# Two heads of the neighbourhood attention on the two column halves of the array, q and k stored as parts, and four smaller moves

## The chip, the cores and the metric

The kernel runs on one core of a Trainium2 chip. The metric is the device time of one execution in microseconds (us). The engines are PE (TensorE; PEld is its weight load), DVE (VectorE), ACT (ScalarE), POOL (GpSimd) and SP, whose queue issues the DMAs.

## The reference, cut to what matters

Two layers over 1024 latent and 256 context tokens of width 1024. Layer 0 mixes with attention: four differential heads over all 1280 keys, and eight neighbourhood heads (width 64) whose queries see an 8 x 16 window of a grid 64 wide plus the 256 context keys:

```python
s = concat([q·k_window * scale + bias, q·k_ctx * scale])   # one softmax over both
p = softmax(s)
out = p[:n_loc] @ v_window + p[n_loc:] @ v_ctx
```

Layer 1 mixes with a recurrent block: a projection, a width-4 convolution, two sigmoid gates for each of two directions, a scan each way, and the product with a GELU lane. Each mixer and each convolutional FFN is modulated by vectors made from `c` by a 1024 x 6144 matrix per layer (`ada_w`), and wrapped in a residual LayerNorm. All is float32.

## The kernel before

Products that need float32 accuracy are made from parts: x = h + l, with h rounded to the array's fast type (`fp32r`) on ACT and l = x - h on DVE or POOL (`split`, L101). A projection then takes three matmuls (`mm3`, L121). The score matmuls of the attention take two, with q's high part in the first 64 rows and its low part in the last 64 (`heads`, L479; `scores`, L531).

Stages in order of time: modulation rows and the v projection; the q/k projection (`qkv`, from L436); the differential units; the neighbourhood units; the output projection (`proj_ln`); the FFN of layer 0; the recurrent block (`rnn`); its output projection; the FFN of layer 1.

*The q/k projection* has 16 blocks of 128 output channels (L446). A block splits its weight (L447: ACT, then POOL), runs 8 x 3 matmuls for each of three column chunks into PSUM banks taken in turn, evicts on ACT into the one tile `q` (L463), rotates the first eight blocks on DVE and POOL (L468 to L471), and stores `q` to DRAM (L472). Three steps of `ada` are laid between: each loads a 512 KB row of `ada_w` through the same ring of three tiles as the weights, and DVE multiplies and sums it twice (L205).

*Heads* are loaded from DRAM ahead of their use, by `ahead`: each of q and k twice, into both halves of the partitions, then cast on DVE (L500, L503) and subtracted on POOL (L501, L505).

*A neighbourhood unit* is one head m of a pair, for 128 queries (j), and is a generator of six steps: scores and the maximum (DVE L1449, L1450); exp on ACT with the sum, and the division of p by it on DVE (L1469); six or seven transposes of p on PE; their eviction; the product with v; its eviction into 64 rows of `o` (L1507). v's 64 columns are the stationary operand, so the product uses 64 columns of the array: columns 0 to 63 for m = 0, the others for m = 1. In each turn of the loop from L587 PE gets the scores of unit i+2, the transposes of i-1 and the product of i-2.

*The recurrent block* makes, for each n of 8, four gate lanes by sigmoid (L1147) from one PSUM region of three banks, then two scans; lanes 2 and 3 have one buffer each (L1122), which n+1 takes after the last reader of n (L1178 on POOL, L1179 on DVE).

Each engine runs its queue in order. The order is chosen by a planner that models times, except where `in_turn` (L90) fixes it: in attention all of PE's, ACT's, DVE's and POOL's instructions are in turn, each on its engine, but not the first weights of the output projection (`w_ao`), which the planner put between the q/k projection and the first differential units. The loads and stores share SP's queue.

Of the kernel before, what the change touches and what calls it, by code (L numbers as in the profile page):

```python
# [26 lines left out]
P = 128  # L27
# [30 lines left out]
class Kernel:  # L58
    def __init__(self, nc, tc, es, a):
        self.nc, self.tc, self.a, self.es = nc, tc, a, es  # L60
        self.turns = {}
        self.pe_key = self.ld_key = None
        self.rooms = 0
        self.cast = None
        self.const = self.pool(es, "const", 1)
# [3 lines left out]
        self.qk_s = [d.tile([P, T], F32, name=f"qk_s{i}", tag=f"qk_s{i}") for i in range(16)]  # L69
# [283 lines left out]
    def qkv(self, esa):  # L353
        nc, a = self.nc, self.a
        with ExitStack() as es:
# [80 lines left out]
            with ExitStack() as es1:  # L436
                qp = self.pool(es1, "qkproj", 1)
                more = self.ada(qp, [(0, p) for p in (2, 3, 4, 5)] + [(1, 0), (1, 1)], 0)
                cos = qp.tile([P, TL], F32, name="cos")
                sin = qp.tile([P, TL], F32, name="sin")  # L440
                cyc = itertools.cycle((4, 6, 7))
                self.spare((5,))
                self.ld(cos, a["cos"])
                self.ld(sin, a["sin"])
                shuf = [(i + 16) % 32 for i in range(32)]
                for n, i in enumerate((0, 4, 1, 5, 2, 6, 3, 7, 8, 12, 9, 13, 10, 14, 11, 15)):  # L446
                    w = self.weight(a["w_qk"][i])  # L447
                    if n == 3:
                        self.pool_p = self.pool(esa, "weights", 1, side="right")
                        self.diff = DiffAttention(self)  # L450
                    if n == 15:

                        cyc = itertools.cycle((6, 7))
                        self.pe_key = "att_pe"
                        self.first = self.diff.unit(0, 0)
                        for _ in range(4):
                            next(self.first)
                    q = qp.tile([P, T], F32, name="q", tag="q")
                    scale = 0.125 if i // 4 in (0, 2) else 1.0
                    for c0, cn in CHUNKS:  # L460
                        ps = self.banks(next(cyc))
                        self.block(ps[:, :cn], w, c0, cn)
                        nc.scalar.mul(q[:, c0:c0 + cn], ps[:, :cn], scale)  # L463
                        if n:
                            next(more, None)
                    if i < 8:
                        rot = qp.tile([P, TL], F32, name="rot", tag="rot")
                        nc.vector.stream_shuffle(rot, q[:, :TL], shuf)  # L468
                        nc.vector.tensor_mul(rot, rot, sin)
                        nc.gpsimd.tensor_mul(q[:, :TL], q[:, :TL], cos)  # L470
                        nc.vector.tensor_add(q[:, :TL], q[:, :TL], rot)  # L471
                    self.st(self.qk_s[i], q)  # L472
                self.pe_key = None
                for _ in more:
                    pass
            self.fold(0, 0, 0, 0, 3, 4)


    def heads(self, n, out, sub=None):  # L479

        nc = self.nc
        pool = self.sets[n % 2]
        iq, ik = (n, 4 + n) if n < 4 else (4 + n, 8 + n)
        parts = []
        v = pool.tile([P, NT, P], F32, name="v", tag="v")
        out.append((parts, v))
        for m in range(2):

            rows = slice(m * 64, m * 64 + 64)
            qr = pool.tile([P, T], F32, name="qr", tag="qr")  # L490
            kr = pool.tile([P, T], F32, name="kr", tag="kr")
            for t_, i in ((qr, iq), (kr, ik)):
                self.ld(t_[0:64], self.qk_s[i][rows])
                self.ld(t_[64:128], self.qk_s[i][rows])
# [4 lines left out]
            yield  # L499
            self.dve(nc.vector.tensor_copy(qs, qr))  # L500
            self.pl(nc.gpsimd.tensor_sub(qs[64:128], qr[64:128], qs[64:128].bitcast(F32)))  # L501
            yield
            self.dve(nc.vector.tensor_copy(kh, kr))  # L503
            if sub is None:
                self.pl(nc.gpsimd.tensor_sub(kl, kr, kh.bitcast(F32)))  # L505
            else:
                sub.tensor_sub(kl, kr, kh.bitcast(F32))
        self.ld(v, self.v_s[:, :, n * P:(n + 1) * P].rearrange("t p e -> p t e"))

    def dve(self, ins):  # L510
# [26 lines left out]
    def attention(self):  # L537
# [3 lines left out]
        with ExitStack() as es:  # L541
# [45 lines left out]
            for i in range(nd, len(units) + 2):  # L587
                s(i + 2)
                if i == nd:
                    s(i - 1)  # L590
                s(i + 1)
                t = i - 1
                if t >= nd:
                    s(t, 2)
                    f(i, 2)
                if i < len(units):
                    n.ahead(*units[i][1:])
                if i == nd:
                    s(nd - 1, 2)
                    done(nd - 1)  # L600
                elif t > nd:
                    s(t - 1, 2)

    def turn_out(self, o, blk, scale, bank):

# [74 lines left out]
    def proj_ln(self, src, w, nk, l, which, nt, x_in, x_out, nx, fold, sizes, more=(), held={},  # L680
# [8 lines left out]
        with ExitStack() as es:  # L689
# [14 lines left out]
            for size in sizes:  # L704
# [11 lines left out]
                for k in range(nk):  # L716
# [3 lines left out]
                    if gt is None and k == (nk - 1 if tail else 0):  # L720
# [6 lines left out]
                    wh, wl = self.weight(w[k], (P, D), nc.vector)  # L727

                    first = early and t0 == 0
                    if tail and t0 == 0:  # L730
# [358 lines left out]
    def rnn(self, left):  # L1089
# [32 lines left out]
        def lane(i, n):  # L1122

            j = {0: 0, 1: 1, 4: 2}.get(i)
            if j is not None and n % 2:
                return self.aring.tile([P, T], F32, name="lane", tag=f"a{j}")
            return self.ln.tile([P, T], F32, name="lane", tag=f"y{i}")

# [8 lines left out]
        def gates(n, g, xs, x, yg):  # L1137
# [157 lines left out]
class DiffAttention:  # L1295
    def __init__(self, kn):
        self.kn = kn
        self.heads, self.outs = [], {}
        for _ in kn.heads(0, self.heads, kn.nc.vector):
            pass  # L1300
        self.next = iter(())

# [9 lines left out]
    def unit(self, h, b):  # L1312
# [35 lines left out]
        wT = pool.tile([P, T], F32, name="wT", tag="wT", bufs=2)  # L1348

        def turn(g):  # L1350
            pt = kn.banks((6, 7, 6)[g])
# [36 lines left out]
class NatAttention:  # L1388
# [42 lines left out]
    def unit(self, pr, j, m):  # L1431
# [35 lines left out]
        for u in range(nu):  # L1467
            sl = slice(u * n // nu, (u + 1) * n // nu)
            kn.dve(nc.vector.tensor_scalar_mul(p[:, sl], p[:, sl], rr[:, u:u + 1]))  # L1469
        yield  # L1470
        pT = pool.tile([P, T], F32, name="wT", tag="wT", bufs=2)
        self.pair = 10 - self.pair
        ba, bb = kn.banks(self.pair), kn.banks(self.pair + 1)
        work = ((ba, 0, 4, 0), (bb, 4, 4 if j == NTL else 2, 4 * P if j == NTL else nr * GW))
# [12 lines left out]
            self.outs[pr] = pool.tile([P, T], F32, name="o", tag="o", bufs=2)  # L1487
        o = self.outs[pr]
        if j == NTL:
            for u in range(4):  # L1490
                hs, qs = slice(u % 2 * 64, u % 2 * 64 + 64), slice(u // 2 * P, u // 2 * P + P)
                for k in range(2):
                    kn.mm(ba[hs, qs], v[:, NTL + k, hs], pT[:, (2 * u + k) * P:(2 * u + k + 1) * P],
                          start=k == 0, stop=k == 1)
            yield
            kn.act(o[:, TL:], ba[:, :TC], AF.Copy)
# [5 lines left out]
        hs = slice(m * 64, m * 64 + 64)  # L1502
# [102 lines left out]
```

## Time and profile before

| | us |
|---|---|
| median of 3 runs | 3009.2 (3004.59 to 3010.11) |
| the profiled execution, its own time | 3005.08 |
| its span | 3003.3 |
| PE busy in the span | 2859.1 (95%) |
| DVE, ACT, POOL busy | 2061.9, 1475.3, 931.3 |

Busy time of PE includes matmuls that run at the lower of its two clocks. The stages need different engines, so each is read by itself, by windows of the trace.

### The profile page before, as it was taken

What the parts mean: (1) busy time and instruction counts of PE and PEld (TensorE: products, weight loads), DVE (VectorE), ACT (ScalarE), POOL (GpSimd) and SP (SyncE); (2) the same over time, 40 slices, a digit from 0 to 9 for tenths busy, and PEclk for the clock granted to TensorE, in tenths of its full rate; (3) what the DMA queues carried; (4) which work ended last, traced back from release to release, by engine and by line L of the source; (5) the groups of instructions that cost most, each with busy time, mean ns of one, the idle gap of its engine ahead of it and who ended that gap; (6) DMA issues with size and microseconds to landing.
All of it is one profiled execution on the core that took longest, in us unless ns stands there. A gap on an engine that the chain in (4) does not pass through costs nothing. (4 is left out here: it accounts for less than half of the span.)

```text
span 3003.3 us, 38303 instructions
## 1 busy us (share of the span) xinstructions
PE 2859.1 (95%) x14430; PEld 2367.8 (79%) x14430; DVE 2061.9 (69%) x2743; ACT 1475.3 (49%) x2358; POOL 931.3 (31%) x636
## 2 busy tenths in 40 slices
PE   8987988889999999999999999999989999999998
PEld 5876777778887888778888888777767888888876
DVE  6079759988866787875556645566688977777364
ACT  4211136666666664344444434466767554454232
POOL 4134204543300015354430000244311366761001
PEclk9998999999999999999999999999989999999999
DMA  6365542223208413632126646311146122225452
GB/s 227 128 183 194 198 158 71 71 62 87 61 29 279 175 63 107 189 119 69 69 77 215 217 158 206 100 49 50 51 164 232 64 84 79 80 77 201 146 196 99
DMA packets 133596, 381.60 MB, mean 127 GB/s; under 512 B 14334, under 2 KB 39966, under 8 KB 133282
## 3 DMA queue, kind: packets, MB, share of 16 engines
q1 hardware_dynamic: 133410, 379.15, 38.2%
q8 instruction: 113, 1.85, 0.3%
q14 instruction: 73, 0.60, 0.1%
HBM read 310.13 MB, written 68.97 MB: 126 GB/s over the span
## 5 line engine op out<-in xcount | busy, mean ns | idle before, releaser
L124 PE MATMUL pb<-wl,a 128*128 128x512 f32 x1040 | 397.6, 393 | 2.7 <-DVE wl L103 2.7
L125 PE MATMUL pb<-wh,a 128*128 128x512 f32 x1040 | 394.8, 392 | 0.8 <-DVE a L103 0.7
L123 PE MATMUL pb<-wh,a 128*128 128x512 f32 x1040 | 387.5, 393 | 7.0 <-ACT a L102 5.1
L102 ACT CAST wh<-wr 128x1024 fp32r<-128x1024 f32 x182 | 191.3, 1051 | 407.3 <-PE pb L124 282.3
L103 DVE TENSOR_TENSOR wl<-wr,wh 128x1024 fp32r<-128x1024 f32 x166 | 202.8, 1223 | 234.5 <-ACT wh L102 233.3
L123 PE MATMUL pb<-hh,wh 128*128 128x512 f32 (+1 forms) x704 | 263.8, 375 | 31.7 <-ACT q L463 31.0
L124 PE MATMUL pb<-hl,wh 128*128 128x512 f32 (+1 forms) x704 | 261.7, 372 | 1.3 <-DVE hl L669 1.3
L125 PE MATMUL pb<-hh,wl 128*128 128x512 f32 (+1 forms) x704 | 261.4, 371 | 0.0
L646 POOL TENSOR_SCALAR s<-s 128x1 f32<-128x1 f32 x36 | 16.0, 446 | 769.6 <-ACT x L645 768.9
L123 PEld LDWEIGHTS pb<-wh,a 128*128 128x128 f32 x1040 | 195.4, 188 | 50.8 <-ACT a L102 6.5
L124 PEld LDWEIGHTS pb<-wl,a 128*128 128x128 f32 x1040 | 195.3, 188 | 44.2 <-DVE wl L103 4.2
L125 PEld LDWEIGHTS pb<-wh,a 128*128 128x128 f32 x1040 | 195.3, 188 | 42.2 <-DVE a L103 2.1
L103 POOL TENSOR_TENSOR wq<-sq,wq 128x512 fp32r<-128x512 f32 x96 | 157.0, 1639 | 193.8 <-ACT wq L102 193.0
L517 ACT ACTIVATE p<-pb,nm 128x1280 f32<-128x1280 f32 (+3 forms) x160 | 158.8, 995 | 67.6 <-DVE nm L1327 65.9
L896 POOL TENSOR_TENSOR sq<-wr 128x512 f32<-128x512 f32 x72 | 120.2, 1669 | 225.4 <-DMA wr<-w_up 216.3
L123 PEld LDWEIGHTS pb<-hh,wh 128*128 128x128 f32 x704 | 137.3, 195 | 55.0 <-ACT q L463 32.7
L852 DVE SCALAR_TENSOR_TENSOR lane<-lane,cv 128x1023 f32<-128x1023 f32 x88 | 128.2, 1459 | 52.2 <-ACT lane L851 51.9
L123 PE MATMUL pb<-t,wq 128*128 128x512 f32 x400 | 157.6, 395 | 4.9 <-DVE lane L1031 4.5
L124 PE MATMUL pb<-t,wq 128*128 128x512 f32 x400 | 157.9, 395 | 0.0
L125 PE MATMUL pb<-t,wq 128*128 128x512 f32 x400 | 157.8, 395 | 0.0
L124 PEld LDWEIGHTS pb<-hl,wh 128*128 128x128 f32 x704 | 137.3, 195 | 23.8 <-DVE hl L669 1.5
L125 PEld LDWEIGHTS pb<-hh,wl 128*128 128x128 f32 x704 | 136.8, 194 | 22.6
(323 smaller groups left out, 7598.0 us busy)
## 6 DMA issues: line engine op xcount, KB each, us to landing
wr<-w_dn SPq DMA_DIRECT2D x110, 512.0 KB, 3.6
wr<-w_up SPq DMA_DIRECT2D x88, 512.0 KB, 3.6
wr<-ada_w SPq DMA_DIRECT2D x80, 512.0 KB, 3.9
ar<-g_s SPq DMA_DIRECT2D x88, 256.0 KB, 3.7
wr<-w_ao SPq DMA_DIRECT2D x32, 512.0 KB, 5.4
g_s<-lane SPq DMA_DIRECT2D x22, 640.0 KB, 3.0
x_s<-y SPq DMA_DIRECT2D x26, 512.0 KB, 6.0
x<-x_s SPq DMA_DIRECT2D x26, 512.0 KB, 5.5
```

Of the source, the lines that this page charges most:

```text
L102: self.cast = self.nc.scalar.copy(h, raw)
L103: (sub or self.nc.vector).tensor_sub(l, raw, h.bitcast(F32))
L123: i = mm(out, a[0], b[0], start=first, stop=False, **kw)
L124: mm(out, a[0], b[1], start=False, stop=False, **kw)
L125: j = mm(out, a[1], b[0], start=False, stop=last, **kw)
L517: self.in_turn("att_act", self.nc.scalar.activation(*args, **kw))
L646: nc.gpsimd.tensor_scalar(rs, sq, 1.0 / D, EPS, op0=ALU.mult, op1=ALU.add)
L852: nc.vector.scalar_tensor_tensor(c[:, 1:], u[:, :n - 1], cvw[:, 0:1], c[:, 1:], op0=ALU.mult, op1=ALU.add)
L896: op(have[n], x, y)
```

## The change

1. *Parts stored.* After the rotation `q` is split into h (ACT) and l (DVE, in place), and both are stored: two stores of 640 KB a block. `heads` loads the parts straight into their tiles, 12 loads of 320 KB a head in place of 8, and has no cast and no subtraction. `q` has two buffers. The weight's l and the product with `cos` go from POOL to DVE.
2. *Two heads on the halves.* p is not divided. The sum's reciprocal is spread by POOL over 64 columns (`rb`); for m = 0 the product is put off; with m = 1 the products of both heads alternate on the two column halves; one full-width matmul of `rb` with the identity turns the reciprocals into rows that fit `o`; ACT copies them into `o`, and DVE multiplies the product into it. `wT` has four buffers.
3. *Rooms.* In `rnn`, lanes 2 and 3 get a second buffer; one addition goes from POOL to DVE.
4. *Early weights in turn.* The first three blocks of `w_ao` are split in the last turns of the attention loop, in ACT's and DVE's order.

```diff
-                    w = self.weight(a["w_qk"][i])
+                    w = self.weight(a["w_qk"][i], sub=nc.vector)
...
-                    q = qp.tile([P, T], F32, name="q", tag="q")
+                    q = qp.tile([P, T], F32, name="q", tag="q", bufs=2)
+                    h = qp.tile([P, T], F32R, name="qh", tag="qh")
...
-                        nc.gpsimd.tensor_mul(q[:, :TL], q[:, :TL], cos)
+                        nc.vector.tensor_mul(q[:, :TL], q[:, :TL], cos)
...
-                    self.st(self.qk_s[i], q)
+                    self.split(q, h, q.bitcast(F32R))
+                    self.st(self.qk_s[i][0], h.bitcast(F32))
+                    self.st(self.qk_s[i][1], q)
...
-            self.dve(nc.vector.tensor_copy(qs, qr))
-            self.pl(nc.gpsimd.tensor_sub(qs[64:128], qr[64:128], qs[64:128].bitcast(F32)))
...
+            for half in range(2):
+                to = slice(half * 64, half * 64 + 64)
+                self.ld(qs[to].bitcast(F32), self.qk_s[iq][half, rows])
+                self.ld(kh[to].bitcast(F32), self.qk_s[ik][0, rows])
+                self.ld(kl[to].bitcast(F32), self.qk_s[ik][1, rows])
+                yield
...
+                if 0 <= i - len(units) + 5 < 3:
+                    self.weight_ahead(i - len(units) + 5)
...
+    def weight_ahead(self, k):
+        raw = self.ring.tile([P, D], F32, name="wr", tag="wr", bufs=3)
+        h, l = (self.ring.tile([P, D], F32R, name="w" + i, tag="wq", bufs=6) for i in "hl")
+        self.ld(raw, self.a["w_ao"][k])
+        self.act(h, raw, AF.Copy)
+        self.dve(self.nc.vector.tensor_sub(l, raw, h.bitcast(F32)))
+        self.ahead[k] = h, l
...
-            if j is not None and n % 2:
+            if j is None and n % 2:
+                return big(f"lane{i}")
+            if n % 2:
...
-                nc.gpsimd.tensor_add(ro, ro, sx[1][:, :TL])
+                nc.vector.tensor_add(ro, ro, sx[1][:, :TL])
...
-            kn.dve(nc.vector.tensor_scalar_mul(p[:, sl], p[:, sl], rr[:, u:u + 1]))
+        kn.pl(nc.gpsimd.tensor_copy(rb[:, m:m + nu], rr.unsqueeze(2).to_broadcast([P, nu, GW])))
...
-        po = bb[hs, 3 * P:]
+        if m == 0:
+            self.first_half = pT
+            return
         for k, (s, n, tb) in enumerate(seq):
-            kn.mm(po, v[:n, tb, hs], pT[:n, s * P:(s + 1) * P], start=k == 0, stop=k == len(seq) - 1)
+            for mm, t_ in enumerate((self.first_half, pT)):
+                hs = slice(mm * GW, mm * GW + GW)
+                kn.mm(bb[hs, 3 * P:], v[:n, tb, hs], t_[:n, s * P:(s + 1) * P],
+                      start=k == 0, stop=k == len(seq) - 1, skip_group_check=True)
+        kn.mm(ba[:, :P], rb[:, :2].rearrange("p a c -> p (a c)"), kn.ident, start=True, stop=True)
         yield
-        kn.act(o[hs, j * P:(j + 1) * P], po, AF.Copy)
+        js = slice(j * P, (j + 1) * P)
+        kn.act(o[:, js], ba[:, :P], AF.Copy)
+        kn.dve(nc.vector.tensor_mul(o[:, js], bb[:, 3 * P:], o[:, js]))
```

## Rows read from the trace of the kernel before

**Rows 1.** Windows by stage: bounds and length in us, busy us (and count) of PE, PEld, DVE, ACT and POOL, granted clock as a share of full speed, busy share of the DMA engines, GB/s. In order: q/k projection, its end, differential units, neighbourhood units, recurrent block.

```profile
151.00:421.00 270.00, 237.38 (x1171) 201.35 (x1169) 196.25 (x237) 45.38 (x71) 75.75 (x24) 0.94 0.54 176
421.00:446.00 25.00, 16.18 (x85) 14.09 (x84) 19.16 (x29) 12.60 (x21) 1.36 (x3) 0.86 0.97 308
446.00:690.00 244.00, 216.33 (x1516) 192.15 (x1514) 224.30 (x308) 161.89 (x363) 119.31 (x135) 0.98 0.25 66
690.00:899.00 209.00, 205.92 (x1566) 174.73 (x1564) 157.36 (x401) 135.19 (x336) 53.71 (x35) 1.00 0.20 58
...
1905.00:2240.00 335.00, 307.28 (x1406) 248.14 (x1405) 221.02 (x250) 220.69 (x206) 120.26 (x52) 0.96 0.24 78
```

**Rows 2.** Matmuls of PE in order of time around the q/k blocks (start us, us; in brackets the idle time before, and what ended it): the first matmul of blocks 0, 1 and 8, and the last one of block 15.

```profile
151.42 0.39 PE L123 MATMUL pb<-hh,wh 128*128 128x512 f32 x1
...
165.17 0.40 PE L123 MATMUL pb<-hh,wh 128*128 128x512 f32 x1
...
295.90 0.80 PE L123 MATMUL pb<-hh,wh 128*128 128x512 f32 x1 [6.82 <-ACT q L463]
...
420.90 0.28 PE L125 MATMUL pb<-hh,wl 128*128 128x256 f32 x1
```

**Rows 3.** Waits in the q/k projection, the last one those of SP's queue (who waited for whom: us in total, times, longest).

```profile
ACT q L463 <- DMA qk_s<-q: 84.1, 10, 16.3
PE pb L123 <- ACT q L463: 31.0, 8, 6.8
SPq L83 <- DVE wr L205: 148.1, 41, 13.0
```

**Rows 4.** DVE's operations of the q/k projection and one cast of ACT: single lines (shortest/median/longest ns), then groups (count, busy us, mean ns of one).

```profile
L205 DVE SCALAR_TENSOR_TENSOR wr<-wr,c_rows x80: 1210/1225/3471, 167.1 to 1309.1; 128x1024 f32<-128x1024 f32 x80
L469 DVE TENSOR_TENSOR rot<-rot,sin x8: 1214/3386/3404, 171.6 to 298.7; 128x1024 f32<-128x1024 f32 x8
L507 DVE TENSOR_TENSOR kl<-kr,kh x2: 1482/2823/4164, 215.7 to 236.7; 128x1280 fp32r<-128x1280 f32 x2
L468 DVE STREAM_SHUFFLE rot<-q 128x1024 f32<-128x1024 f32 x8 | 11.0, 1370 | 0.0
L205 DVE DVE_READ_ACCUMULATOR pb<-wr,c_rows 128x1 f32 x47 | 6.5, 139 | 0.0
L102 ACT CAST hh<-x_raw 128x1280 fp32r<-128x1280 f32 x4 | 5.0, 1261 | 0.8 <-DVE x_raw L415 0.8
```

**Rows 5.** DVE and POOL in order of time in a stretch of 7 us of the q/k projection.

```profile
244.25 3.47 DVE L205 SCALAR_TENSOR_TENSOR wr<-wr,c_rows 128x1024 f32<-128x1024 f32 x1
...
244.23 2.41 POOL L103 TENSOR_TENSOR wl<-wr,wh 128x1024 fp32r<-128x1024 f32 x1 [12.66 <-ACT wh L102]
246.59 3.38 POOL L470 TENSOR_TENSOR q<-q,cos 128x1024 f32<-128x1024 f32 x1
```

**Rows 6.** In order of time, at the end of the q/k projection: the first units and a `w_ao` cast.

```profile
436.36 1.04 ACT L102 CAST wh<-wr 128x1024 fp32r<-128x1024 f32 x1 [5.30 <-DMA wr<-w_ao]
...
437.96 2.37 PE L520 MATMUL pb<-v,wT 128*128 128x128 f32 x11 [4.87 <-ACT wT L517]
```

**Rows 7.** PE's waits in the differential units.

```profile
PE pb L523 <- DVE o L1373: 9.4, 13, 1.5
PE pb L523 <- DVE p L1344: 7.2, 9, 1.2
```

**Rows 8.** Groups of DVE and POOL in the differential units (count, busy us, mean ns), and one L1339 while POOL was idle.

```profile
L1339 DVE SCALAR_TENSOR_TENSOR cf<-ss,nlam,rr 128x1 f32<-128x1 f32 x29 | 28.0, 965 | 1.0
L1373 DVE TENSOR_SCALAR o<-pb,rr 128x128 f32<-128x128 f32 x39 | 13.1, 344 | 5.9 <-PE pb L520 5.6
L500 DVE CAST qs<-qr 128x1280 fp32r<-128x1280 f32 x9 | 7.3, 816 | 0.0
...
L505 POOL TENSOR_TENSOR kl<-kr,kh 128x1280 fp32r<-128x1280 f32 x9 | 26.3, 2918 | 17.3 <-DVE rr L1338 15.8 <-DVE kh L503 1.5
...
442.58 0.22 DVE L1339 SCALAR_TENSOR_TENSOR cf<-ss,nlam,rr 128x1 f32<-128x1 f32 x1
```

**Rows 9.** PE in order of time: a differential product of full width (20 records for ten matmuls); transposes and product of a neighbourhood unit with seven key tiles, and the next scores; a context unit, whose product changes halves after each 4 records, and the next scores; a product with six key tiles, and the next scores.

```profile
445.33 2.39 PE L520 MATMUL pb<-v,wT 128*128 128x128 f32 x20
...
699.87 1.88 PE L520 MATMUL pb<-wT,v 128*64 128x128 f32 x14
701.68 0.50 PE L520 MATMUL pb<-kh,qs 128*128 128x512 f32 x1
...
729.91 1.14 PE L520 MATMUL pb<-wT,v 128*64 128x128 f32 x16
730.98 0.42 PE L520 MATMUL pb<-kh,qs 128*128 128x320 f32 x1
...
732.60 1.52 PE L520 MATMUL pb<-wT,v 128*64 128x128 f32 x12
734.05 0.41 PE L520 MATMUL pb<-kh,qs 128*128 128x320 f32 x1
```

**Rows 10.** The recurrent block: a wait of ACT (total, times, longest), the one of PE behind it, and one such wait of PE in order of time.

```profile
ACT lane L1120 <- DVE lane L1179: 26.3, 7, 4.8
...
PE pb L123 <- ACT lane L1120: 17.9, 9, 3.4
...
1990.45 0.50 PE L123 MATMUL pb<-xh,wg 128*128 128x512 f32 x1 [2.69 <-ACT lane L1120]
```

More of the change, by code (lines that the diff above doesn't have):

```diff
@@ L64, in __init__ @@
         self.cast = None
+        self.ahead = {}
         self.const = self.pool(es, "const", 1)
@@ L68, in __init__ @@
         d = es.enter_context(tc.tile_pool(name="dram", bufs=1, space=DRAM))
-        self.qk_s = [d.tile([P, T], F32, name=f"qk_s{i}", tag=f"qk_s{i}") for i in range(16)]
+        self.qk_s = [d.tile([2, P, T], F32, name=f"qk_s{i}", tag=f"qk_s{i}") for i in range(16)]
         self.v_s = d.tile([NT, P, D], F32, name="v_s", tag="v_s")
@@ L476, in qkv, with heads @@
             self.fold(0, 0, 0, 0, 3, 4)
-    def heads(self, n, out, sub=None):
-        nc = self.nc
+    def heads(self, n, out):
         pool = self.sets[n % 2]
@@ L489, in heads @@
             rows = slice(m * 64, m * 64 + 64)
[L490 to L494, printed above, removed]
             qs = pool.tile([P, T], F32R, name="qs", tag=f"qs{m}")
@@ L726, in proj_ln @@
                             gi = self.ln_vecs(pool, *norm_in, "in")
-                    wh, wl = self.weight(w[k], (P, D), nc.vector)
+                    wh, wl = self.ahead.pop(k, None) or self.weight(w[k], (P, D), nc.vector)
                     first = early and t0 == 0
@@ L1298, in __init__ @@
         self.heads, self.outs = [], {}
-        for _ in kn.heads(0, self.heads, kn.nc.vector):
+        for _ in kn.heads(0, self.heads):
             pass
@@ L1347, in unit @@
         pool = kn.pool_a
-        wT = pool.tile([P, T], F32, name="wT", tag="wT", bufs=2)
+        wT = pool.tile([P, T], F32, name="wT", tag="wT", bufs=4)
         def turn(g):
@@ L1466, in unit @@
         kn.dve(nc.vector.reciprocal(rr, ss))
-        for u in range(nu):
-            sl = slice(u * n // nu, (u + 1) * n // nu)
-            kn.dve(nc.vector.tensor_scalar_mul(p[:, sl], p[:, sl], rr[:, u:u + 1]))
+        if m == 0:
+            self.rb = pool.tile([P, 4, GW], F32, name="rb", tag="rb", bufs=3)
+        rb = self.rb
+        kn.pl(nc.gpsimd.tensor_copy(rb[:, m:m + nu], rr.unsqueeze(2).to_broadcast([P, nu, GW])))
         yield
-        pT = pool.tile([P, T], F32, name="wT", tag="wT", bufs=2)
+        pT = pool.tile([P, T], F32, name="wT", tag="wT", bufs=4)
         self.pair = 10 - self.pair
@@ L1489, in unit @@
         if j == NTL:
-            for u in range(4):
-                hs, qs = slice(u % 2 * 64, u % 2 * 64 + 64), slice(u // 2 * P, u // 2 * P + P)
+            for t in range(2):
+                qs = slice(t * P, t * P + P)
                 for k in range(2):
-                    kn.mm(ba[hs, qs], v[:, NTL + k, hs], pT[:, (2 * u + k) * P:(2 * u + k + 1) * P],
-                          start=k == 0, stop=k == 1)
+                    for m in range(2):
+                        hs, u = slice(m * GW, m * GW + GW), 2 * t + m
+                        kn.mm(ba[hs, qs], v[:, NTL + k, hs], pT[:, (2 * u + k) * P:(2 * u + k + 1) * P],
+                              start=k == 0, stop=k == 1, skip_group_check=True)
+                kn.mm(bb[:, qs], rb[:, 2 * t:2 * t + 2].rearrange("p a c -> p (a c)"), kn.ident,
+                      start=True, stop=True)
             yield
-            kn.act(o[:, TL:], ba[:, :TC], AF.Copy)
+            kn.act(o[:, TL:], bb[:, :TC], AF.Copy)
+            kn.dve(nc.vector.tensor_mul(o[:, TL:], ba[:, :TC], o[:, TL:]))
             kn.st(kn.att_s[4 + pr], o)
@@ L1501, in unit @@
             seq.append((6, 64, r0 // 2 + 4))
-        hs = slice(m * 64, m * 64 + 64)
-        po = bb[hs, 3 * P:]
+        if m == 0:
+            self.first_half = pT
+            return
         for k, (s, n, tb) in enumerate(seq):
-            kn.mm(po, v[:n, tb, hs], pT[:n, s * P:(s + 1) * P], start=k == 0, stop=k == len(seq) - 1)
+            for mm, t_ in enumerate((self.first_half, pT)):
[3 more added lines that the diff above has]
+        kn.mm(ba[:, :P], rb[:, :2].rearrange("p a c -> p (a c)"), kn.ident, start=True, stop=True)
         yield
-        kn.act(o[hs, j * P:(j + 1) * P], po, AF.Copy)
+        js = slice(j * P, (j + 1) * P)
+        kn.act(o[:, js], ba[:, :P], AF.Copy)
+        kn.dve(nc.vector.tensor_mul(o[:, js], bb[:, 3 * P:], o[:, js]))
 def _blocks(w, n):
```

7 lines of the change are left out of this document (removed).

## The prediction

> **What bounds the kernel now.** I read the windows by stage first, then in each stage that the change touches the waits of PE, the groups of the engine that they point to, and PE's order of time.
>
> PE is busy 95% of the span, but not evenly. In the neighbourhood units it is 205.9 of 209 us at the full clock, the level of 2.4 GHz: they are bound by PE, and only less PE work makes them shorter [rows 1]. In the q/k projection PE idles 270 - 237.4 = 32.6 us, in its end 8.8, in the differential units 27.7, in the recurrent block 27.7 [rows 1]. The granted clock is below 1.00 in just these four, 0.94 in the first: after such gaps some matmuls run at 1.2 GHz.
>
> In the q/k projection PE waits 31.0 us for ACT's evictions, and ACT waits 84.1 us for the store of the one `q` tile [rows 3]. The store waits for the rotation, which DVE and POOL do between the `ada` sums. DVE is slowed by POOL: one multiply-and-sum took 3.47 us beside two POOL operations, where the shortest of the same shape took 1.21, and the product with `sin` took 3.39 at the median against 1.21 [rows 4, 5]. So a subtraction on POOL costs DVE more than doing it itself. Blocks 1 to 7 took 295.9 - 165.2 = 130.7 us, 18.7 each, and blocks 8 to 15 took 421.2 - 295.9 = 125.3; block 0, which ran without a gap, took 13.75 [rows 2].
>
> **The change part by part.**
>
> *q/k projection.* DVE's work for a block with rotation is afterwards: shuffle 1.37, three products and sums of 1.21 (`sin`, `cos`, add) 3.63, the new subtraction on 128 x 1280 1.48 (the shortest L507), the weight's l 1.21, and six `ada` sums of 1.21 with their read-outs (0.14 and some 0.08 in turn) 7.9: 15.6 us [rows 4]. That is over PE's 13.75, so blocks 1 to 7 stay DVE's, at 15.6 plus some 3% for DMA waits, 16.1: 7 x (18.7 - 16.1) = 18. Blocks 8 to 15 need 1.48 + 1.21 + 7.9 = 10.6 of DVE, so PE's 13.75 sets them; with two `q` tiles the wait for the store goes, and 125.3 falls toward 110. I take 117, a gain of 8, as the rotated blocks leave DVE a backlog. ACT's new casts (16 of 1.26, as [rows 4] has for this shape) fit: ACT is busy 45 of 270 us. But an eviction now stands behind the cast, and the cast behind the rotation; what is late next is the rotation, not the store. The second store is 16 x 640 KB = 10.5 MB; the stage moves 176 GB/s at a DMA share of 0.54 [rows 1], so full use would be some 326 GB/s (an estimate from that row), and 10.5 MB are 32 us of 270, a share of 0.66. SP issues 16 stores more, which wait for a cast or a subtraction with loads queued behind. I take 25 for the stage; bounds 3 (DVE is no faster, its sum of work stays near the 196 that it has now) and 38 (PE's 16 x 13.75 = 220 with 12 lost, against 270).
>
> *End of the projection.* The planner had put a `w_ao` cast before an eviction of the first unit; the cast waited 5.3 us for its DMA, and PE 4.87 for that eviction, while DMA was 0.97 busy [rows 1, 6]. In turn at the end of attention this cannot be. Head 1 loads 12 x 320 KB in place of 8, 1.3 MB more, but three blocks of 512 KB leave. Gain 5 (0 to 8.8). The three casts and subtractions come back late in attention, 1.04 on ACT and 1.21 on DVE each, in turns where ACT has room (135 of 209); cost 0 to 3, in the 5.
>
> *Differential units.* DVE is busy 224 of 244 us and PE's waits are DVE's: 9.4 + 7.2 [rows 1, 7]. The loads of q and k take 18 casts of 0.82 off DVE = 14.7, and 18 operations of 2.92 off POOL = 52.5. What POOL's company cost DVE: L1339 takes 0.22 alone and 0.965 at the mean, 29 x 0.74 = 21.6 [rows 8]. So DVE falls by some 36, to 188, below PE's 216. The 16.6 us of waits go nearly all, with some of the clock's 2% (5 us): I take 18 (8 to 25). What is left late are the evictions of the turned outputs.
>
> *Neighbourhood units.* Before, a product with six key tiles is 12 records in 734.05 - 732.60 = 1.45 us, one with seven 1.81 [rows 9]. The context unit shows what two halves give: its 16 records change halves after each four, and took 1.07, 0.067 a record against 0.121. So 24 records of a pair take 1.61 in place of 2.90, and 28 take some 2.01 (the 64-row ones cost 0.36 of a unit; 0.40 for a pair) in place of 3.62. The `rb` matmul adds 2 records of full width, 2 x 0.12 by the differential product (20 in 2.39). Gain per pair 1.05 or 1.37, and of each kind there are 16: 38.7; less 8 such matmuls in the context units, 1.9: 36.8 us of PE.
>
> Can the others keep up? PE's 206 fall to 169. DVE's 157 lose the divisions and gain 36 products of 0.344 [rows 8]; even with no division counted off it is 169. ACT's 135 gain nothing. But the new stage is uneven: a turn without a product is followed by one with two, and the transposes two units on wait until ACT has read `rb` from their bank. I take 0.2 us for a pair, 6.4: gain 30 (10 to 38; below nothing only if the halves don't overlap). POOL's spreads are off PE's path, with a whole turn to land.
>
> The Trainium skill, "TensorE: Matmul & The Clock Gate", Part 3 (The mechanism), says that a weight load overlaps matmuls in flight only when the row group differs; halves by columns share theirs. By that sentence the second head's loads would stand between the matmuls and the stage would gain nothing. The same part's table has three column tiles at 2.38x, and the context unit's 0.067 sides with the table.
>
> *Recurrent block.* ACT waits 26.3 us in 7 waits for the last reader of lane 2, and PE is held by ACT 17.9 in all, 2.69 in the one shown [rows 10]. With a second room the wait has no object; POOL's addition is also gone from that chain. Next late is the PSUM region itself, one for four gates. PE's gaps there with their colder matmuls: gain 13 (4 to 20). The output projection, both FFNs and the rest are bound by PE and unchanged.
>
> Sum: 25 + 5 + 18 + 30 + 13 = 91. The profiled execution took 3005.1, its span 1.8 less; 3005.1 - 91 = 2914. The median of the runs lies 4.1 above it, so 2918 for a median.
>
> **Rivals.**
>
> 1. *DVE keeps the pace of the projection.* What moves from POOL and the new subtraction cost 16 x (1.48 + 1.21) + 8 x 1.21 = 53 us of DVE, against POOL's company, whose price I only have from some rows. For it: DVE's sum stays; against: its mean durations are far over the shortest. The stage gains 3: 2940.
> 2. *ACT and DVE pace the neighbourhood units.* The uneven turns put a stall of 0.8 us on each pair (32 x 0.8 = 26 of the 36.8). For it: the bank wait above; against: ACT and DVE idle a quarter of the stage. The units gain 10: 2938.
> 3. *The halves don't run at once*, so the change doesn't do what it says: no gain on products, 32 x 0.24 + 1.9 = 9.6 lost: 2918 + 30 + 10 = 2958. The context unit speaks against it.
> 4. *Slower: SP's queue.* It already stands 148.1 us on DVE for the ring of loads, up to 13.0 at a time [rows 3]. If each block's stores, waiting for a subtraction that DVE does only after six sums (7.9 + 1.48 + ACT's 1.26 = 10.6), stand ahead of the loads that those sums need, each of 15 blocks loses 10.6, 159 us, and the projection's 25 is not had: 2918 + 25 + 159 = 3102. It decides from (91 - 25) / 15 = 4.4 us a block. Against it: the planner places a store by when it expects its data.
>
> **How the numbers follow.** Forecast 0.62; rival 1 0.16, rival 2 0.11, rival 3 0.03, rival 4 0.05; 0.03 for mixtures of 1 and 2 with less elsewhere. The time is the likeliest's, 2918. The best ends, 38 + 8 + 25 + 37 + 18, are 126 (2883), unlikely together; the range is 2890 to 2960, and leaves out rival 4 and the extremes. The runs shown differ by under 0.2%, about what can be told from no change, so same means within 6 us: 0.01. Slower 0.05 (rival 4), faster 0.94.
>
> **What would show it.** In the q/k projection: no wait of ACT for `qk_s`, no DVE operation of 3.4 us, blocks 1 to 7 at 16 us. No cast of `w_ao` near its end. In the differential units PE idle under 12 us. In the neighbourhood units 24 records in 1.6 us and pairs 1.0 to 1.4 shorter, without transposes that wait. In the recurrent block no wait for L1179's successor. A projection of 270 us or longer, or 24 records in 2.9, would make the prediction wrong.

## The result, and the profile after

The median after is 2884.3 us (2881.91 to 2887.59, four runs) against 3009.48 beside it: a ratio of 0.9588, 95% interval 0.9572 to 0.9605. The gain is 125 us where 91 was forecast, and the time lies under the range, which began at 2890.

Stage by stage, each from the first matmul of its own kind to the first of the next (the neighbourhood units and the recurrent block to their last one; the bounds differ from [rows 1] by up to 37 us), in us:

| stage | before | after | gain | forecast |
|---|---|---|---|---|
| q/k projection and its end | 286.6 | 247.7 | 38.9 | 30 |
| differential units | 236.3 | 203.1 | 33.2 | 18 |
| neighbourhood units | 224.1 | 177.6 | 46.5 | 30 |
| output projection and FFN of layer 0 | 1043.4 | 1047.9 | -4.5 | 0 |
| recurrent block | 263.6 | 245.5 | 18.1 | 13 |
| its output projection | 134.4 | 140.4 | -6.0 | 0 |
| FFN of layer 1, and ahead of the q/k projection | 814.9 | 817.8 | -2.9 | 0 |

Windows after, the answer to [rows 1] (same columns): q/k projection, its end, differential units, neighbourhood units, recurrent block, its output projection.

```profile
150.80:385.70 234.90, 229.56 (x1167) 196.30 (x1166) 187.43 (x266) 65.48 (x86) 0.00 (x0) 0.97 0.73 243
385.70:398.50 12.80, 8.70 (x38) 6.57 (x37) 12.52 (x21) 5.90 (x10) 0.00 (x0) 0.87 0.89 225
398.50:601.60 203.10, 197.74 (x1458) 181.44 (x1456) 177.12 (x270) 158.59 (x351) 66.76 (x124) 1.00 0.54 131
601.60:779.20 177.60, 175.27 (x1751) 151.78 (x1750) 115.59 (x377) 134.08 (x328) 38.01 (x89) 1.00 0.40 102
1827.10:2072.60 245.50, 241.95 (x1156) 200.28 (x1155) 186.91 (x148) 181.59 (x157) 86.57 (x34) 0.99 0.18 61
2072.60:2213.00 140.40, 126.94 (x546) 99.42 (x545) 108.70 (x166) 90.59 (x149) 16.29 (x18) 0.95 0.57 192
```

In the first five lines PE's busy time is now within 6 us of the length. The last line lost 6.0: PE is busy 126.9 of 140.4, where it had been busy 127.1 of 134.4, as the same stage in the kernel before shows:

```profile
2205.40:2339.80 134.40, 127.10 (x557) 100.28 (x556) 108.58 (x166) 91.33 (x150) 15.74 (x18) 0.95 0.57 202
```

Waits in the q/k projection after, against [rows 3]: ACT's for the store fell from 84.1 to 20.6, and PE's for ACT from 31.0 to 0.9; what PE still waits longest for is one weight's l.

```profile
ACT q L465 <- DMA qk_s<-q: 20.6, 4, 8.3
PE pb L126 <- DVE wl L104: 2.6, 1, 2.6
PE pb L124 <- ACT q L465: 0.9, 1, 0.9
SPq L84 <- DVE wr L206: 89.2, 38, 13.0
```

The blocks, from first matmul to first matmul: 13.75, 13.8, 15.7, 18.2, 19.6, then 13.8 to 14.0 each, but 16.1 for block 14, in which the first scores stand. DVE in order of time in block 1 (start, us):

```profile
167.01 1.40 DVE L470 STREAM_SHUFFLE rot<-q 128x1024 f32<-128x1024 f32 x1
168.30 1.23 DVE L206 SCALAR_TENSOR_TENSOR wr<-wr,c_rows 128x1024 f32<-128x1024 f32 x1
169.45 0.09 DVE L206 DVE_READ_ACCUMULATOR wr<-wr,c_rows 128x1 f32 x1
169.45 1.23 DVE L206 SCALAR_TENSOR_TENSOR pb<-wr,c_rows 128x1024 f32<-128x1024 f32 x1
170.60 0.15 DVE L206 DVE_READ_ACCUMULATOR pb<-wr,c_rows 128x1 f32 x1
170.60 1.23 DVE L471 TENSOR_TENSOR rot<-rot,sin 128x1024 f32<-128x1024 f32 x1
171.73 1.22 DVE L472 TENSOR_TENSOR q<-q,cos 128x1024 f32<-128x1024 f32 x1
```

An operation of 1.23 us is followed by the next after 1.15, and the read-out of a sum begins together with the next operation: here it costs nothing.

PE in the neighbourhood units after (start, us; x28 are the records of a pair with seven key tiles):

```profile
662.01 0.93 PE L519 MATMUL pb<-ident,p 128*128 128x128 f32 x7
662.71 0.41 PE L516 MATMUL pb<-kh,qs 128*128 128x320 f32 x1
...
663.58 0.93 PE L519 MATMUL pb<-ident,p 128*128 128x128 f32 x7
664.44 1.90 PE L516 MATMUL pb<-wT,v 128*64 128x128 f32 x28
666.27 0.49 PE L516 MATMUL pb<-ident,rb 128*128 128x128 f32 x2
666.51 0.48 PE L516 MATMUL pb<-kh,qs 128*128 128x512 f32 x1
...
680.05 1.53 PE L516 MATMUL pb<-wT,v 128*64 128x128 f32 x24
681.51 0.49 PE L516 MATMUL pb<-ident,rb 128*128 128x128 f32 x2
```

28 records stand from 664.44 to 666.27, 1.83 us; 24 take 1.46; the two of `rb` 0.24. Seven transposes keep PE 0.70 us when scores follow (662.01 to 662.71) and 0.86 when a product does (663.58 to 664.44). In the whole stage the means are 0.71 (15 times) and 0.86 (14 times); for six transposes they are 0.67 and 0.75.

### The profile page after: what moved, and what is told of

Its sections match the earlier page's. It is cut to its first block, busy times and chain, and to the rows that moved or that the text cites. A ratio compares the mean times of both kernels' runs of the same rounds, so it can differ in the third digit from the quotient of the medians.

```text
span 2880.0 us, 38562 instructions
## 1 busy us (share of the span) xinstructions
PE 2794.1 (97%) x14510; PEld 2322.9 (81%) x14510; DVE 1978.0 (69%) x2712; ACT 1484.9 (52%) x2342; POOL 759.2 (26%) x643
## 4 chain that ended last, share of the span: by engine, by line
PE 78%; DVE 8%; issue 3%; ACT 2%; DMA 2%; POOL 1%; SPq 0%; DVEq 0%; ACTq 0%; POOLq 0%
PE pb L126 22%; PE pb L125 22%; PE pb L124 22%; PE pb L516 8%; PE pb L519 3%; DVE nm L1336 1%; DMA wr<-ada_w 1%; DVE wr L206 1%; DVE y L825 1%; DVE lane L861 0%; ACT p L513 0%; DVE p L1353 0%; DVE y L650 0%; DVE lane L859 0%; PE pb L276 0%
## 5 line engine op out<-in xcount | busy, mean ns | idle before, releaser
L104 DVE TENSOR_TENSOR wl<-wr,wh 128x1024 fp32r<-128x1024 f32 x179 | 218.4, 1221 | 272.0 <-ACT wh L103 269.8
L125 PEld LDWEIGHTS pb<-wl,a 128*128 128x128 f32 x1040 | 196.2, 189 | 45.7 <-DVE wl L104 5.5
L104 POOL TENSOR_TENSOR wq<-sq,wq 128x512 fp32r<-128x512 f32 x96 | 151.1, 1577 | 203.2 <-ACT wq L103 202.5
L903 POOL TENSOR_TENSOR sq<-wr 128x512 f32<-128x512 f32 x72 | 123.3, 1712 | 226.8 <-DMA wr<-w_up 218.9
```

Source lines behind the costliest of these rows:

```text
L104: (sub or self.nc.vector).tensor_sub(l, raw, h.bitcast(F32))
L125: mm(out, a[0], b[1], start=False, stop=False, **kw)
L903: op(have[n], x, y)
```

## The experiments

All start from the changed kernel. Each was compared with the kernel before on the same chip.

### Each part undone by itself

*Old products* brings back the division of p, one product for each head, and no `rb`.

> Part 2 alone undone: p is divided on DVE and each head's product runs by itself, wT keeps four buffers, all else as changed. Theory A (the change's gain falls by stage as the two traces stand: 224.1 us of neighbourhood units became 177.6, and that is all the halves'): 46.5 us slower than the changed kernel, about 2931 us, with the units back at 224. Rival B (the casts that left DVE and POOL's part in these units gave some of it): the units come to some 214, 2920 us. Rival C (the uneven turns had cost stalls that this takes away, so the halves were worth more in PE work): PE's records alone, 36.8 us slower, 2921.

Measured 2925.6 (2923.1 to 2926.3): the neighbourhood units take 221.9 in place of 177.6, all else stays within 2. By its stage that is nearest to theory A; the total lies between A's 2931 and the 2920 and 2921 of the rivals. The part is worth 41 in the median and 44 in its stage.

*Old heads* stores q alone, and casts and subtracts in attention again (POOL subtracts).

> The stored parts alone undone: q is stored whole, heads are cast on DVE and subtracted on POOL as before; q's two buffers and DVE's work in the projection stay. Theory A (POOL's company on DVE was the whole of the differential units' loss): the differential units go back from 203 us to about 236, and the projection gains some of the 12 us that blocks 2 to 4 lose beside the loads, so 25 to 33 us slower than the changed kernel, 2910 to 2917. Rival B (the forecast's 18, and the rest of the differential units' gain came from the four buffers of wT and the early weights): the differential units at some 218, 2899.

Measured 2916.0 (2914.6 to 2921.7). The differential units take 234.1, 31 us more: nearly the whole gain of that stage. Theory A. The projection with its end gains 5.7 by it, and the neighbourhood units lose 5.5.

*Old rooms* takes the second buffers of lanes 2 and 3 away; the addition stays on DVE.

> The second rooms of gate lanes 2 and 3 alone undone; the addition stays on DVE. Theory A (the room's wait was PE's gap): the gaps of 2.1 to 2.7 us a block come back, a bit shorter for the addition on DVE (1.2 in place of 2.4), 12 to 18 us slower than the changed kernel, 2896 to 2902. Rival B (the addition on POOL was the wait): at most 5 us slower, 2889. Both theories leave the loss after the recurrent block (some 6 us) open: if it comes from the rooms, it goes here.

Measured 2882.6 (2881.7 to 2884.8): no loss, which of the two totals only rival B's allows. But the recurrent block takes 253.4 in place of 245.5, so the rooms are worth 7.9 there; the other 10 of the 18 are the addition's by difference, as it was not undone alone. Against that, its output projection takes 133.1 in place of 140.4. The rooms' gain is given back in the next stage.

*Old weights* leaves the first `w_ao` weights to the planner.

> The early weights alone undone: the planner places the first w_ao casts where it likes. Theory A (they stood in the way at the end of the projection): that end is 5 us longer again, 2889 us. Rival B (with POOL free and other loads, the planner places them elsewhere): no difference, 2884, within 3 us.

Measured 2895.3 (2891.0 to 2901.4), past both numbers. Two waits of the profiled run, the slowest of the four, just as the differential units begin:

```profile
ACT wh L103 <- DMA wr<-w_ao: 13.7, 2, 13.4
PE pb L519 <- DVE o L1380: 13.4, 1, 13.4
```

The planner puts the cast into the same kind of place as before, ahead of the first unit's evictions; its weight now comes 13.4 us late, not 5.3 [rows 6], and PE stands for all of it. The edit doesn't earn these 11 us against the kernel before; it keeps the other parts from making an old wait worse.

### The q/k projection: POOL or the store?

```diff
# pool_split
-                    w = self.weight(a["w_qk"][i], sub=nc.vector)
+                    w = self.weight(a["w_qk"][i])
...
-                        nc.vector.tensor_mul(q[:, :TL], q[:, :TL], cos)
+                        nc.gpsimd.tensor_mul(q[:, :TL], q[:, :TL], cos)
# one_q
-                    q = qp.tile([P, T], F32, name="q", tag="q", bufs=2)
+                    q = qp.tile([P, T], F32, name="q", tag="q")
```

> The changed kernel with the subtraction of each q/k weight and the product with cos back on POOL; two q tiles and the stored parts stay. Theory A (POOL's company is what slowed DVE, and DVE what held the projection): of the 34 us that the projection gained most goes back, since DVE's multiply-and-sum again has POOL beside it in every block: stage 219 to about 245, a median of about 2910. Rival B (the wait of the single q tile for its store was the loss, and two tiles remove it): the stage stays within 4 us of 219, a median of 2884 to 2889.

> The changed kernel with a single q tile; the work on DVE and the stored parts stay. Theory A (POOL's company): q is stored sooner because DVE is faster, the stage stays within 6 us of 219, a median of 2884 to 2891. Rival B (the store's wait): ACT's evictions wait for the store of q again, some 84 us of ACT as before, of which PE felt some 31: stage about 245, a median of about 2910.

POOL's work back: 2899.6 (2897.0 to 2904.1), the stage 232.6 (219.1 in the changed kernel, up to the first scores; 253.5 before). One `q` tile: 2916.9 (2915.2 to 2921.7), the stage 253.2. Rival B holds for the second run, and most of A's price was not found in the first: a single tile alone puts the stage back to where it was, with nothing on POOL, and POOL's work costs 13.5. So the single tile hid POOL's company: the move from POOL gains nothing without the second tile. The reverse does not hold: the second tile gains 20.9 of the 34.4 with POOL's work still there. (The single tile is held longer here than before, for a cast, a subtraction and a second store, so that 253.2 comes so close to 253.5 may be partly chance.) With POOL's work DVE's multiply-and-sums into `pb` take 1666 ns at the mean, against 1231 in the changed kernel:

```profile
L206 DVE SCALAR_TENSOR_TENSOR pb<-wr,c_rows 128x1024 f32<-128x1024 f32 x47 | 78.3, 1666 | 108.1 <-ACT c_rows L193 92.9 <-DMA wr<-ada_w 15.1
```

Waits with one tile:

```profile
ACT q L465 <- DMA qk_s<-q: 78.6, 14, 9.8
PE pb L124 <- ACT q L465: 34.0, 8, 8.8
```

These are nearly [rows 3] again.

### The product: do two halves run at once?

```diff
# one_half
-                kn.mm(bb[hs, 3 * P:], v[:n, tb, hs], t_[:n, s * P:(s + 1) * P],
+                to = bb[:GW, 3 * P:] if mm == 0 else ba[:GW, P:2 * P]
+                kn.mm(to, v[:n, tb, hs], t_[:n, s * P:(s + 1) * P],
# head_outer
-        for k, (s, n, tb) in enumerate(seq):
-            for mm, t_ in enumerate((self.first_half, pT)):
+        for mm, t_ in enumerate((self.first_half, pT)):
+            for k, (s, n, tb) in enumerate(seq):
```

> The changed kernel with both heads' products of a neighbourhood pair on columns 0 to 63 (the second to another bank), so that rows 64 to 127 of o are neither multiplied nor mixed; one small DVE product more for a pair. The weight loads, the columns and the number of records stay. Theory A (the second head is hidden because it stands on the other half of the columns): a record takes some 0.12 again in place of 0.065, 24 take 2.9 and 28 some 3.4, 1.3 to 1.6 us more for each of 32 pairs, 46 us: a median of about 2930. Rival B (narrow records cost half wherever they stand): a median of 2884 to 2890.

> The changed kernel with the records of a pair in another order: all six or seven of head 0, then all of head 1. Theory A (two halves overlap only where neighbouring records stand on different halves): the overlap is left at one place of a pair, some 0.11 a record, 24 in 2.7 us, a loss of 1.1 to 1.4 us for each of 32 pairs, 40 us: a median of about 2924. Rival B (runs of several records on one half still overlap with the next run, as the context unit of before showed with runs of four at 0.067 a record): a median of 2884 to 2890.

On one half: 2942.3 (2940.7 to 2943.9). Heads one after the other: 2930.1 (2927.9 to 2930.8). A product with six key tiles in each (one half first):

```profile
706.25 2.83 PE L516 MATMUL pb<-wT,v 128*64 128x128 f32 x24
709.02 0.49 PE L516 MATMUL pb<-ident,rb 128*128 128x128 f32 x2
```

```profile
704.07 2.46 PE L516 MATMUL pb<-wT,v 128*64 128x128 f32 x24
706.46 0.49 PE L516 MATMUL pb<-ident,rb 128*128 128x128 f32 x2
```

24 records take 2.77 on one half, 2.39 in two runs of 12, and 1.46 alternating. So the halves run at once, and rival B fails both times. The starts of the single records show how: alternating, one record of each half starts, 7 ns apart, and such a pair every 0.109 us; on one half a single record starts every 0.109 us. (One half paid some 12 us more for its extra product: PE waited 11.9 for it, 29 times.)

That only direct neighbours overlap, as theory A of the second run has it, is not shown. In the pair above head 1's first record starts at 705.00, when three of head 0's are still to start (the last at 705.33), and the context unit of before, with runs of four, took 0.067 a record [rows 9]. So records overlap across some three or four places of the order. With seven key tiles the same run gains nothing, and passes the 3.34 that 28 records take on one half, which is why its total lies over theory A's 2924:

```profile
621.89 3.70 PE L516 MATMUL pb<-wT,v 128*64 128x128 f32 x28
625.51 0.49 PE L516 MATMUL pb<-ident,rb 128*128 128x128 f32 x2
```

There each head's run ends with its two records of 64 rows; the record after a change of rows starts 0.20 us later and not 0.109, and the two runs don't overlap. That the change of rows is the reason is inferred.

### The differential units: POOL's company or the casts?

*heads_dve* is the old heads with the subtractions on DVE; the other two add to the changed kernel the old work of one engine alone, into a tile that nobody reads.

```diff
# heads_dve, against old_heads
-            self.pl(nc.gpsimd.tensor_sub(qs[64:128], qr[64:128], qs[64:128].bitcast(F32)))
+            self.dve(nc.vector.tensor_sub(qs[64:128], qr[64:128], qs[64:128].bitcast(F32)))
# pool_company (more_casts: two DVE copies of qs and kh instead)
+            if n:
+                dum = pool.tile([P, T], F32, name="dum", tag="dum")
+                self.pl(self.nc.gpsimd.tensor_sub(dum[64:128], qs[64:128].bitcast(F32), kh[64:128].bitcast(F32)))
+                self.pl(self.nc.gpsimd.tensor_sub(dum, kh.bitcast(F32), kl.bitcast(F32)))
```

> The changed kernel with the stored parts undone (the casts of q and k again in attention, as in the run with the parts undone, which took 2916.0 and 234.1 in the differential units), but with the subtractions of those parts on DVE in place of POOL. Theory A (POOL's company was the greater price of the old form): DVE has its 177 of now, 18 casts of 0.82 and 18 subtractions of some 1.48, 218 us, all beside no POOL work: the stage falls from 234 to 218 to 224, a median of 2902 to 2906. Rival B (company costs little, and DVE only pays for what it does itself): 18 x 1.48 = 27 us more on an engine that already sets the pace, the stage rises to 250 to 261, a median of 2932 to 2943.

Measured 2920.9 (2920.9 to 2923.5), between the two: the differential units take 226.9, 7 less than with POOL, but the neighbourhood units 199.4, as DVE pays there for its own. It did not decide.

> The changed kernel, with the two subtractions that the old form gave POOL for each half head done again on POOL, into a tile that nobody reads; the stored parts are loaded as they are, and DVE gets no work. Theory A (POOL's company was most of the 31 us that the old form costs in the differential units, through DVE's operations beside it): DVE's busy time rises from 177 to 200 to 215, the stage from 203 to 220 to 230, a median of 2901 to 2912. Rival B (it was the casts on DVE): the stage stays under 208, a median of 2884 to 2890.

> The changed kernel, with two casts of 0.82 on DVE for each half head, into a tile that nobody reads, and no work for POOL. Theory A (the casts alone fit into DVE's slack): stage 203 to 207, a median of 2884 to 2889. Rival B (the casts were most of the 31 us, since DVE's answers to PE stand behind them): stage 215 to 225, a median of 2896 to 2906.

POOL's work alone: 2907.2 (2903.2 to 2909.7), the stage 229.6, 26.5 more. The casts alone: 2892.0 (2887.8 to 2892.6), the stage 208.3, 5.2 more. Together 31.7, close to the 31.1 that undoing the part cost in this stage: theory A in the first, and nearer to A in the second. DVE is then busy 203.6 us with POOL's work, in place of 177.1: 26.5 more, just what the stage lost. The window of the stage and DVE's groups (count, busy us, mean ns):

```profile
396.50:626.10 229.60, 208.02 (x1456) 187.33 (x1454) 203.64 (x270) 159.96 (x351) 115.76 (x140) 0.97 0.49 117
```

```profile
L1340 DVE TENSOR_REDUCE nm<-pb 128x1 f32<-128x1280 f32 (+1 forms) x67 | 93.0, 1389 | 8.8 <-PE pb L520 8.5
L1357 DVE SCALAR_TENSOR_TENSOR p<-p,cf 128x512 f32<-128x512 f32 (+1 forms) x70 | 78.2, 1117 | 0.0
L1352 DVE SCALAR_TENSOR_TENSOR cf<-ss,nlam,rr 128x1 f32<-128x1 f32 (+1 forms) x34 | 18.5, 544 | 1.2
L1386 DVE TENSOR_SCALAR o<-pb,rr 128x128 f32<-128x128 f32 x40 | 13.4, 342 | 6.6 <-PE pb L520 6.3
```

The same groups in the changed kernel:

```profile
L1336 DVE TENSOR_REDUCE nm<-pb 128x1 f32<-128x1280 f32 (+1 forms) x67 | 93.2, 1390 | 8.5 <-PE pb L516 7.4
L1353 DVE SCALAR_TENSOR_TENSOR p<-p,cf 128x512 f32<-128x512 f32 (+1 forms) x70 | 60.1, 859 | 0.0
L1348 DVE SCALAR_TENSOR_TENSOR cf<-ss,nlam,rr 128x1 f32<-128x1 f32 (+1 forms) x34 | 8.7, 256 | 1.2
L1382 DVE TENSOR_SCALAR o<-pb,rr 128x128 f32<-128x128 f32 x40 | 13.5, 344 | 4.2 <-PE pb L516 3.6
```

DVE's own list is the same, yet `p` takes 18.1 us more and `cf` 9.8, while the two forms that read PSUM do not move. PE's own busy time is 10 us more for the same matmuls, at a granted clock of 0.97 in place of 1.00. The Trainium skill, "SBUF — State Buffer" (Who interferes with whom), says that a DVE instruction with two SBUF inputs contends with a GpSimd instruction that reads SBUF, and one with at most one SBUF input, outside the modes that use both ports, does not. These four groups agree.

### The loss after the recurrent block

```diff
# rooms_not_last
-            if j is None and n % 2:
+            if j is None and n % 2 and n < KD - 1:
                 return big(f"lane{i}")
-            if n % 2:
+            if j is not None and n % 2:
```

> The changed kernel with the second room of the gates for blocks 1, 3 and 5 only; block 7 takes the first one again. Theory A (the output projection's gate, vector and row tiles lie on the memory of the last block's rooms, so that their loads wait for the last store; this gives back the rooms' gain): the output projection falls from 140.4 to 133 to 135, the recurrent block pays one wait, 1 to 2 us: a median of 2877 to 2881. Rival B (the output projection simply takes over the time by which the recurrent block ends sooner): 140 stays, a median of 2884 to 2887.

Measured 2873.8 (2872.7 to 2877.7), a ratio of 0.9562 (0.9536 to 0.9588): 10.5 us under the changed kernel and below theory A's total, the best of all. The output projection takes 132.7, 7.7 less; the recurrent block 245.8, 0.3 more. SP's queue in the changed kernel, and then in this one (start, us, number of issues):

```profile
2102.49 0.33 SPq L89 DMA_DIRECT2D r_s<-lane  x1
2102.86 0.43 SPq L84 DMA_DIRECT2D g<-gate_s  x1
2103.34 1.58 SPq L84 DMA_DIRECT2D in<-lnv  x2
2104.96 2.87 SPq L84 DMA_DIRECT2D x<-x_s  x4
```

```profile
2088.64 0.43 SPq L84 DMA_DIRECT2D g<-gate_s  x1
2089.12 1.05 SPq L84 DMA_DIRECT2D in<-lnv  x2
2090.21 1.42 SPq L84 DMA_DIRECT2D x<-x_s  x3
...
2102.80 0.32 SPq L89 DMA_DIRECT2D r_s<-lane  x1
```

With the last block on the new rooms, the next stage's loads come only behind the last store; without, 14 us ahead of it. Theory A's placement is shown. That it is the tiles' memory, and not another reason of the planner, is inferred from the edit.

### The three slow blocks that are left

> The changed kernel with the first head's parts loaded from the sixth block of the projection on, not from the fourth. Theory A (the 12 us that blocks 2 to 4 take over PE's 13.75 come from these loads standing ahead of the blocks' own on a busy DMA, wherever they are put): the loss moves with the loads, q/k stage 217 to 221, a median of 2882 to 2887. Rival B (it comes from their falling on blocks with rotation, whose DVE has no slack; at the sixth and seventh half of it stays): stage 212 to 216, a median of 2877 to 2881.

> The changed kernel with the first head's parts loaded from the ninth block on, where no rotation is left. Theory A (the loss goes with the loads): stage 217 to 221, a median of 2882 to 2887. Rival B (it needs the blocks with rotation): DVE has 3 us of slack in each block from the ninth on, the 12 us fall to 2, stage 208 to 211, a median of 2872 to 2877.

Measured 2882.7 (2881.0 to 2885.3) and 2882.3 (2878.9 to 2883.2). Neither tells anything of the theories: the code moved (`if n == 3` to 5 and 8), but with it at 8 the loads still stood between 180 and 225 us. Their place in SP's queue is the planner's.

```diff
# order_late
-                for n, i in enumerate((0, 4, 1, 5, 2, 6, 3, 7, 8, 12, 9, 13, 10, 14, 11, 15)):
+                for n, i in enumerate((1, 5, 2, 6, 3, 7, 0, 4, 8, 12, 9, 13, 10, 14, 11, 15)):
...
-                    if n == 3:
+                    if n == 8:
```

> The changed kernel with the first head's q and k blocks as the seventh and eighth, and its parts loaded from the ninth on; in the two runs that only moved the code of those loads, the loads themselves stayed between 180 and 225 us, as they wait for nothing but these two blocks. Theory A (these loads fill the DMA in blocks 2 to 4 and cost the 12 us there): moved behind block 7, where DVE has 3 us of slack a block, the stage falls from 219 to 208 to 213, a median of 2873 to 2879. Rival B (the stores and the ring's own loads fill it, or the loads cost as much later): stage 216 to 222, a median of 2881 to 2888.

> The later first head and the rooms for blocks 1, 3 and 5 together. The rooms in that form gave 10.5 alone. Theory A of the later head: 8 us more, a median of 2864 to 2869. Rival B: nothing more, 2872 to 2877.

Measured 2894.1 (2893.0 to 2897.1), and 2884.5 (2878.5 to 2886.9) with the rooms: 10 slower than without it each time. Windows of the first run, to the eighth block and from there on:

```profile
151.20:249.20 98.00, 97.16 (x508) 83.34 (x507) 82.22 (x113) 26.92 (x36) 0.00 (x0) 1.00 0.61 206
249.20:319.70 70.50, 59.96 (x290) 50.60 (x289) 54.95 (x81) 15.16 (x20) 0.00 (x0) 0.90 0.90 289
```

Blocks 2 to 4 ran at 13.8; blocks 8, 9 and 10 took 17.0, 23.3 and 16.1. The loss goes with the loads, as theory A has it, and it is no smaller where DVE has slack, as the second half of rival B has it; the stage took 223.9 up to the first scores, over both ranges. The DMA is 0.90 busy in these 70 us, 0.61 before them; in blocks 2 to 4 of the changed kernel it was 0.99. Only 5.0 of the 10 us lie in the projection and its end. The FFN of layer 0 and the recurrent block's output projection took 3.5 and 3.0 more; the edit does not touch them, and why they differ stays open. Some other spreading of these loads was not tried.

## Why the prediction was wrong

The mechanisms were right: what bounds each stage, the direction of each part, and the rivals' failure (the projection is not held at DVE's old pace, no stall of the bank, no queue of SP). The sizes failed. The four terms were too small by 8.9, 15.2, 16.5 and 5.1 us, and three losses of 4.5, 6.0 and 2.9 were not foreseen: 91 + 45.7 - 13.4 = 123.3, the gain of the span. The differential and the neighbourhood units went beyond their own best ends, 25 and 38. So the gains together passed the best ends that the range left out as "unlikely together", and only the losses brought the time back to 2884. (That sum of best ends has 37 and 18 where the terms say 38 and 20; with these it is 129 and 2880, not 126 and 2883.)

*Neighbourhood units, "I take 0.2 us for a pair".* This step failed by the most, 46.5 for 30. The stall did not come: PE idles 2.3 us in the whole stage. The gain in PE's work was also undersized: 24 records took 1.46, not 1.61, and 28 took 1.83, not 2.01, 16 x (0.15 + 0.18) = 5.3; and half the transposes are now followed by scores in place of a product, which by the means above saves 0.15 with seven tiles and 0.08 with six, 16 x 0.23 = 3.7, which no term had. 36.8 + 5.3 + 3.7 = 45.8 for 46.5 measured. By the sentence of the Trainium skill, "TensorE: Matmul & The Clock Gate", Part 3 (The mechanism), on weight loads and row groups, the alternating order would have gained nothing; it took 0.061 us a record against 0.115 on one half, so the sentence does not hold for column halves here.

*Differential units, "the 16.6 us of waits go nearly all, with some of the clock's 2%".* This step failed next, 33.2 for 18. It named two of PE's waits and 5 us of clock. Nearly all of PE's idle time went, 27.3 to 5.4, and its busy time for the same matmuls fell from 209.1 to 197.7 as the granted clock rose from 0.97 to 1.00: 21.9 and 11.3. That DVE falls by some 36 was near: 217.8 to 177.1.

*q/k projection, "blocks 1 to 7 stay DVE's, at 15.6 plus some 3%".* This step failed too. Adding row durations counted 0.06 to 0.08 us too much for each operation, and the read-outs, which lie inside the next one. By starts a block needs ten operations at 1.15, the shuffle at 1.3 (167.01 to 168.30 above) and the subtraction at some 1.4: 14.2 us, an estimate, and not 15.6. Blocks 1 and 5 to 7 ran at PE's 13.8; in 5 to 7 DVE was busy all the time as well, 41.4 of 41.4 us, so there both set the pace. Blocks 2 to 4, beside the first head's loads, took 15.7 to 19.6, which the 3% for DMA waits did not have. Blocks 1 to 7 gained 22.0 for 18, blocks 8 to 15 12.8 for 8. The reason behind it was weighed wrongly too: the sentence that the rotation, not the store, is late next gave the second `q` tile too little; without it all of the stage's gain is lost, and it brings 20.9 of the 34.4 with POOL's work still there. The end gained 4 for 5.

*Recurrent block.* 18.1 for 13, inside its bounds: PE's idle time fell from 17.9 to 3.6. "The output projection, both FFNs and the rest are bound by PE and unchanged" failed for the projection behind it: the rooms' 7.9 were spent on loads that came 14 us later. The -4.5 of the FFN of layer 0 and the -2.9 stay open; the former's length is 1045.6 to 1051.4 in runs that change nothing there.

## What to carry to other kernels

A stage can be held by two faults, of which one hides the other: undo each by itself before giving one the credit, and count a stall's colder matmuls with it. Add DVE's work from start to start, not from row durations. More buffers in one stage can delay the next stage's loads: look at where in the DMA queue they stand, not only at the waits that went.

## What was not expected of the hardware

POOL's company costs DVE by the operands: two-input forms in SBUF went from 256 to 544 and from 859 to 1117 ns at the mean, forms reading PSUM stayed at 1390 and 344. The column halves run at once, at 0.061 us a record alternating, 0.067 in the old runs of four, 0.100 in runs of twelve and 0.115 on one half, but not across a change of rows: 0.129 in runs of fourteen. And seven transposes hand over to a product 0.15 us later than to scores, at the mean.
